# Weight pieces of 1024 columns instead of 2048 in a two-layer hybrid trunk

## The chip, the cores and the metric

The kernel runs on one core of a Trainium2 chip. The metric is the device time of one execution in microseconds; the median of several runs counts. The engines named here are TensorE (PE; its weight loads are PEld), VectorE (DVE), ScalarE (ACT), GpSimd (POOL) and SyncE (SP), which issues most DMA transfers.

## The reference

The kernel computes `DEPTH` = 2 layers on 256 tokens of width 1024 in float32, then a last RMS norm:

```python
for l in range(DEPTH):
    x = x + 0.5 * swiglu(rmsnorm(x, g_ffn1[l]), w_ffn1_gu[l], w_ffn1_down[l])
    x = x + hybrid_mixer(rmsnorm(x, g_mix[l]), w_in[l], ..., w_out[l], cos, sin)
    x = x + 0.5 * swiglu(rmsnorm(x, g_ffn2[l]), w_ffn2_gu[l], w_ffn2_down[l])
return rmsnorm(x, g_final)
```

The feed-forward width is 2816. The mixer projects to three kinds of attention (six forgetting heads, five stick-breaking heads, five sparse heads whose keys are chosen by an indexer with a top-k of 64) and three gates; each branch is projected up to 1024 columns, gated, summed and projected once more. All weights, about 208 MB, are read from HBM once.

## The kernel before

**Weights.** Every weight matrix is cut into chunks of 256 to 512 columns (the list `chunks`, 101 of them), and a chunk along its rows into blocks of 128, called k. One DMA transfer brings up to four k-blocks of a chunk (eight if the chunk has 256 columns), at most 2048 columns of float32 per partition, into one of four buffers `raw` (`emit_raw`, L223). The first chunk is transferred in smaller parts (the `cuts` of L206) into a buffer of its own, `raw_first`, and the second chunk in parts of two, two and four k-blocks.

**Splits.** The matrix multiplies run in float16, three for each product: a weight is the sum of a high part `whi` and a low part `wlo`, and so are the activations (`xThi`, `xTlo`). `emit_piece` (L258) makes both parts of a piece by `split` (L249): ScalarE scales and rounds `raw` into `whi` (L251), and VectorE subtracts that from the scaled `raw` into `wlo` (L253) and also sums the low part for a check, which is read by a DVE_READ_ACCUMULATOR. A piece is what one such pair of instructions covers: here the whole of a transfer. There are seven pairs of buffers of 2048 columns (`HL_BUFS`, `PIECE`).

**Order.** `project_T` (L317) and `project` (L363) walk over the pieces of a chunk. At the start of each piece they call `advance` (L274), which emits the splits up to `HL_BUFS` pieces ahead and the transfers up to four ahead of the last split, so a split waits for the pair of buffers that TensorE has just finished with. Then come the matmuls, k by k; after every second k-block (every fourth where a chunk has at most 256 columns) and at the end of a piece, `background` (L307) runs one step of each pending side task: attention heads, indexer, norm statistics. The tile framework then fixes the order of the instructions on each engine when the program is built, from their order in the program and its own estimate of when they are ready; on the chip each engine works through its queue in that order.

**What else stands in the same queues.** VectorE and ScalarE also make the operands of the attention (`Ta`, `Wa`, `Tiq`: L818 to L836), softmax parts (`nxa` L1006, `pa` L786, `pTa` L1019), the stick-breaking weights (`eb` L1101), the top-k selection (L915, L916), the gated merge (`gt` L1174 and L1177, `mT` L1179 by way of L251 and L253), the residual and the norm's operands (`xT`, `xThi` L495, `xTlo` L496), and the gate products of the feed-forward (`s0`, L660). At the start `FirstNorm.begin` (L596) alternates the blocks of the first norm with the first splits, as long as fewer than `HL_BUFS` pieces are emitted.

**The check.** `Guard` (L59) keeps one column of sums for each split; `verdict` (L83) transposes them on TensorE 128 columns at a time and reduces them on VectorE near the end. If it fails, a second pass in higher precision (`wide`) follows; it doesn't run here.

Of the kernel before, what the change touches and what calls it, by code (L numbers as in the profile page):

```python
# [24 lines left out]
DEPTH = 2  # L25
# [92 lines left out]
@with_exitstack  # L118
def tile_trunk(ctx, tc, io, out):

    pool = ctx.enter_context(tc.tile_pool(name="gp", bufs=1))
    flag = pool.tile([P, 2], I32, tag="flag", name="flag")
    trunk(tc, io, out, flag)
    bad = tc.nc.values_load(flag[:1, :1], min_val=0, max_val=1)
    with tc.If(bad != 0):
        trunk(tc, io, out, None)
# [3 lines left out]
def trunk(ctx, tc, io, out, flag):  # L130


    nc = tc.nc
    wide = flag is None
    DT = F32R if wide else F16
    sw, sx, sy, sm = (1.0,) * 4 if wide else (SW, SX, SY, SM)
    cp = ctx.enter_context(tc.tile_pool(name="cp", bufs=1))
    wp = ctx.enter_context(tc.tile_pool(name="wp", bufs=1))
    sp = ctx.enter_context(tc.tile_pool(name="sp", bufs=1))
    pp = ctx.enter_context(tc.tile_pool(name="pp", bufs=1, space=PSUM))  # L140
    guard = None if wide else Guard(nc, cp, flag, 256, 80, 3 * DEPTH)

    def behind(i, *firsts):

# [51 lines left out]
            add("w_out", D, h * 512, 512)  # L196
        add_ffn("w_ffn2_gu", "w_ffn2_down")

    RAW, PIECE = 2048, 1024 if wide else 2048
    RAW_BUFS, HL_BUFS = (4, 6) if wide else (4, 7)  # L200
    raws, pieces, chunk_pieces = [], [], []
    for ci, (nm, l, r, c, n) in enumerate(chunks):
        nk = -(-r // P)
        rk = 4 if n > 256 else 8
        pk = rk // 2 if wide else rk
        cuts = [0, 1, 2, 3, 4, 6, 8] if ci == 0 else [0, 2, 4, 8] if ci == 1 else list(range(0, nk, rk)) + [nk]  # L206
        lst = []
        for k0, k1 in zip(cuts, cuts[1:]):
            ks = list(range(k0, k1))
            raws.append((ci, ks))  # L210
            for i in range(0, len(ks), pk):
                sub = ks[i:i + pk]
                lst.append(len(pieces))
                pieces.append((len(raws) - 1, i, len(sub), r // P if r % P else None, sub))
        chunk_pieces.append(lst)
        if ci == 0:
            cuts0 = len(raws)
# [1038 lines left out]
```

## Time and profile before

| | before |
|---|---|
| median of 3 runs | 1148.99 us (1148.11 to 1150.2) |
| the profiled execution | 1148.52 us |
| its span, first to last instruction | 1146.6 us |
| busy PE / DVE / ACT | 1114.1 / 773.9 / 617.6 us |
| `wlo` on VectorE, `whi` on ScalarE (from `raw`) | 217 and 217 instructions |
| DMA | 209.96 MB, mean 183 GB/s |

A busy engine is one that has an instruction at work; matmuls overlap, so a busy share near 100% means that TensorE hardly ever stands still, not that it is at its peak. A wait is idle time of an engine just before an instruction, put down to the instruction that released it last. What TensorE waits for can lengthen the time; what an engine with idle time waits for can't by itself.

### The profile page before, as it was taken

The page shows a single profiled execution, that of the slowest core. Times are in us where ns is not written, and L with a number is a line of the kernel's source. Part 1 is how long each engine was busy: PE and PEld are TensorE (multiplying, and loading weights), DVE is VectorE, ACT ScalarE, POOL GpSimd, SP SyncE. Part 2 cuts the span into 40 slices and gives each one's busy share as a digit, 9 for nine tenths or more (in the row PEclk, how much of TensorE's full clock was granted, in tenths as well). Part 3 has the DMA queues.
Part 4 walks back from the last instruction along what each step waited for, and adds up shares of the span by engine and source line. Part 5 has one row for each costly group of instructions (what it writes and reads, how often), then busy time and mean ns, then how long its engine had stood idle before and what let it go on. Part 6 is the DMA issues. An engine that isn't in the chain of part 4 may idle for free. (4 is left out here: it accounts for less than half of the span.)

```text
span 1146.6 us, 22811 instructions
## 1 busy us (share of the span) xinstructions
PE 1114.1 (97%) x9744; PEld 956.8 (83%) x9744; DVE 773.9 (67%) x1339; ACT 617.6 (54%) x832; POOL 10.0 (1%) x25
## 2 busy tenths in 40 slices
PE   8999999989999999999999999999999999999996
PEld 7888887777888888888888888868788888888765
DVE  6966656897576975565576474579966689565632
ACT  7735445677667554353454363366766665544420
POOL 0000000000000000000000000000000000000000
PEclk9999999999999999999999999999999999999998
DMA  9956655555333865476665565565543439545701
GB/s 324 357 169 219 207 172 165 189 186 172 109 107 123 269 230 170 163 243 200 219 188 180 164 225 175 179 191 191 175 129 111 148 115 321 180 143 199 248 29 41
DMA packets 118755, 209.96 MB, mean 183 GB/s; under 512 B 4802, under 2 KB 43892, under 8 KB 118644
## 3 DMA queue, kind: packets, MB, share of 16 engines
q1 hardware_dynamic: 118324, 207.88, 55.8%
q8 instruction: 78, 1.28, 0.5%
q10 hardware_dynamic: 320, 0.53, 0.1%
q14 instruction: 33, 0.27, 0.1%
HBM read 207.35 MB, written 1.05 MB: 182 GB/s over the span
## 5 line engine op out<-in xcount | busy, mean ns | idle before, releaser
L253 DVE SCALAR_TENSOR_TENSOR wlo<-raw,whi 128x2048 f16<-128x2048 f32 (+5 forms) x217 | 446.4, 2059 | 257.7 <-ACT whi L251 257.5
L339 PEld LDWEIGHTS <-whi 128*128 128x128 f16 x5504 | 536.8, 98 | 67.8 <-issue 4.9
L251 ACT ACTIVATE whi<-raw 128x2048 f16<-128x2048 f32 (+5 forms) x217 | 373.6, 1725 | 384.1 <-issue 95.7
L339 PEld LDWEIGHTS <-wlo 128*128 128x128 f16 x2768 | 270.8, 98 | 38.6 <-issue 4.9
L339 PE MATMUL gw_ffn_gu<-xTlof,whi 128*128 128x256 f16 x704 | 191.7, 273 | 1.2 <-DVE xTlof L496 1.2
L339 PE MATMUL gw_ffn_gu<-xThif,wlo 128*128 128x256 f16 x704 | 191.5, 273 | 1.4 <-DVE wlo L253 1.3
L339 PE MATMUL gw_ffn_gu<-xThif,whi 128*128 128x256 f16 x704 | 191.6, 273 | 0.9 <-DVE s0w_ffn_gu L660 0.9
L339 PE MATMUL uw_ffn_gu<-xThif,whi 128*128 128x256 f16 x704 | 191.9, 273 | 0.0
L339 PE MATMUL uw_ffn_gu<-xThif,wlo 128*128 128x256 f16 x704 | 191.9, 273 | 0.0
L339 PE MATMUL uw_ffn_gu<-xTlof,whi 128*128 128x256 f16 x704 | 191.9, 273 | 0.0
L339 PE MATMUL gt<-xThimx,whi 128*128 128x256 f16 x384 | 104.8, 273 | 0.0
L339 PE MATMUL gt<-xTlomx,whi 128*128 128x256 f16 x384 | 104.7, 273 | 0.0
L339 PE MATMUL gt<-xThimx,wlo 128*128 128x256 f16 x384 | 104.7, 273 | 0.0
L339 PE MATMUL d0w_ffn_down<-ahw_ffn_gu,whi 128*128 128x256 f16 x264 | 72.0, 273 | 0.0
L339 PE MATMUL d0w_ffn_down<-alw_ffn_gu,whi 128*128 128x256 f16 x264 | 72.0, 273 | 0.0
L339 PE MATMUL d0w_ffn_down<-ahw_ffn_gu,wlo 128*128 128x256 f16 x264 | 72.0, 273 | 0.0
L339 PE MATMUL d512w_ffn_down<-ahw_ffn_gu,whi 128*128 128x256 f16 x264 | 72.0, 273 | 0.0
L339 PE MATMUL d512w_ffn_down<-alw_ffn_gu,whi 128*128 128x256 f16 x264 | 72.0, 273 | 0.0
L339 PE MATMUL d512w_ffn_down<-ahw_ffn_gu,wlo 128*128 128x256 f16 x264 | 72.0, 273 | 0.0
L339 PE MATMUL in<-xThimx,wlo 128*128 128x256 f16 x176 | 48.0, 273 | 0.0
L339 PE MATMUL in<-xThimx,whi 128*128 128x256 f16 x176 | 48.0, 273 | 0.0
L339 PE MATMUL in<-xTlomx,whi 128*128 128x256 f16 x176 | 48.0, 273 | 0.0
(329 smaller groups left out, 1372.5 us busy)
## 6 DMA issues: line engine op xcount, KB each, us to landing
raw<-in_w_ffn_gu_dram SPq DMA_DIRECT2D x61, 1024.0 KB, 5.3
raw<-in_w_ffn_down_dram SPq DMA_DIRECT2D x39, 1024.0 KB, 5.1
raw<-in_w_in_dram SPq DMA_DIRECT2D x26, 1024.0 KB, 5.1
raw<-in_w_ffn_gu_dram SPq DMA_DIRECT2D x32, 768.0 KB, 4.7
raw<-in_w_in_dram SPq DMA_DIRECT2D x12, 768.0 KB, 4.4
raw<-in_w_out_dram SPq DMA_DIRECT2D x8, 1024.0 KB, 5.1
raw<-in_w_ffn_down_dram SPq DMA_DIRECT2D x7, 512.0 KB, 3.8
raw<-in_w_in_dram SPq DMA_DIRECT2D x4, 896.0 KB, 4.8
```

Source lines behind the costliest of these rows:

```text
L251: a = nc.scalar.activation(hv, src, AF.Copy, scale=scale)
L253: return a, nc.vector.scalar_tensor_tensor(lv, src, scale, plain(hv), op0=ALU.mult, op1=ALU.subtract, **more)
L339: m = nc.tensor.matmul(o, u, v[:, k, :], start=(k == 0 and q == 0 and b % 2 == 0), stop=(end and q == len(ops) - 1))
```

## The change

`PIECE` becomes 1024 columns in this pass too, and `HL_BUFS` 14 instead of 7: a transfer of up to 2048 columns is now split in two pieces of half as many k-blocks, each with its own `whi` and `wlo` instruction and its own pair of buffers. `advance` is called at each of the smaller pieces. Transfers and `raw` buffers stay as they are. The sums of the check get room for 512 splits.

```diff
-    guard = None if wide else Guard(nc, cp, flag, 256, 80, 3 * DEPTH)
+    guard = None if wide else Guard(nc, cp, flag, 512, 80, 3 * DEPTH)
...
-    RAW, PIECE = 2048, 1024 if wide else 2048
-    RAW_BUFS, HL_BUFS = (4, 6) if wide else (4, 7)
+    RAW, PIECE = 2048, 1024
+    RAW_BUFS, HL_BUFS = (4, 6) if wide else (4, 14)
...
         rk = 4 if n > 256 else 8
-        pk = rk // 2 if wide else rk
+        pk = rk // 2
```

## Rows read from the trace of the kernel before

**Rows 1.** The page, part 1: busy us (share of the span) and instructions per engine.
```profile
PE 1114.1 (97%) x9744; PEld 956.8 (83%) x9744; DVE 773.9 (67%) x1339; ACT 617.6 (54%) x832; POOL 10.0 (1%) x25
```

**Rows 2.** TensorE's waits: who waited for whom: us in total, times, longest us.
```profile
PE sa L860 <- ACT pa L786: 4.1, 2, 2.1
PE o L339 <- DVE mT L253: 2.8, 2, 1.4
PE is L860 <- DVE Tiq L819: 2.3, 2, 1.2
PE sa L860 <- DVE Wa L836: 1.9, 2, 1.2
PE sb L860 <- DVE eb L1101: 1.9, 2, 0.9
...
PE gw_ffn_gu L339 <- DVE wlo L253: 1.3, 3, 0.6
PE gw_ffn_gu L339 <- DVE xTlof L496: 1.2, 3, 0.8
PE ya L990 <- ACT pTa L1019: 1.0, 2, 0.5
PE gw_ffn_gu L339 <- DVE s0w_ffn_gu L660: 0.9, 1, 0.9
...
PE sc L860 <- ACT pa L786: 0.7, 2, 0.4
```

**Rows 3.** Timeline of TensorE: start us, us, instruction [idle before <- releaser].
```profile
15.71 0.28 PE L339 MATMUL gw_ffn_gu<-xThif,wlo 128*128 128x256 f16 x1 [0.60 <-DVE wlo L253]
```

**Rows 4.** Timelines of VectorE and TensorE, first layer's attention.
```profile
248.34 2.29 DVE L253 SCALAR_TENSOR_TENSOR wlo<-raw,whi 128x2048 f16<-128x2048 f32 x1
...
250.67 0.42 DVE L1006 TENSOR_REDUCE nxa<-sa 128x1 f32<-128x256 f32 x1
...
251.75 0.39 PE L860 MATMUL sa<-Wa,Ta 128*128 128x256 f32 x1 [2.07 <-ACT pa L786]
```

**Rows 5.** Timeline of VectorE, second layer, between the merge and the output projection.
```profile
941.56 2.28 DVE L253 SCALAR_TENSOR_TENSOR wlo<-raw,whi 128x2048 f16<-128x2048 f32 x1
...
943.77 0.68 DVE L253 SCALAR_TENSOR_TENSOR mT<-gt,mT 128x512 f16<-128x512 f32 x1
```

**Rows 6.** Groups on VectorE by form: count | busy us, mean ns | idle before, releaser.
```profile
L253 DVE SCALAR_TENSOR_TENSOR wlo<-raw,whi 128x2048 f16<-128x2048 f32 x134 | 306.3, 2289 | 139.7 <-ACT whi L251 139.6
L253 DVE SCALAR_TENSOR_TENSOR wlo<-raw,whi 128x1536 f16<-128x1536 f32 x58 | 101.9, 1757 | 78.2 <-ACT whi L251 78.2
...
L253 DVE SCALAR_TENSOR_TENSOR wlo<-raw,whi 128x1024 f16<-128x1024 f32 x9 | 11.0, 1224 | 9.6 <-ACT whi L251 9.6
```

**Rows 7.** Timeline of VectorE: splits with no idle time between them and the next.
```profile
17.51 1.22 DVE L253 SCALAR_TENSOR_TENSOR wlo<-raw,whi 128x1024 f16<-128x1024 f32 x1
...
18.65 0.48 DVE L496 SCALAR_TENSOR_TENSOR xTlof<-xpf,gT,xThif 128x256 f16<-128x256 f32 x1
...
945.20 2.29 DVE L253 SCALAR_TENSOR_TENSOR wlo<-raw,whi 128x2048 f16<-128x2048 f32 x1
...
947.41 2.29 DVE L253 SCALAR_TENSOR_TENSOR wlo<-raw,whi 128x2048 f16<-128x2048 f32 x1
```

**Rows 8.** Windows: length, busy us of PE, PEld, DVE, ACT, POOL; clock, DMA share, GB/s.
```profile
225.00:250.00 25.00, 24.68 (x225) 21.58 (x223) 24.60 (x63) 18.25 (x34) 0.00 (x0) 1.00 0.62 207
375.00:400.00 25.00, 23.46 (x214) 20.90 (x215) 24.85 (x33) 15.14 (x14) 0.00 (x0) 1.00 0.81 266
```

**Rows 9.** Windows 225:250, 375:400, 787:812, 937:962, instructions on `wlo` alone, their sum.
```profile
sum 100.00, PE 75.30 PEld 26.15 DVE 51.31; mean PE 18.83 PEld 6.54 DVE 12.83
```

**Rows 10.** Groups on ScalarE by form, columns as in rows 6.
```profile
L251 ACT ACTIVATE whi<-raw 128x2048 f16<-128x2048 f32 x134 | 255.2, 1910 | 219.8 <-issue 51.6 <-PE uw_ffn_gu L339 35.8 <-PE gw_ffn_gu L339 34.0
```

**Rows 11.** Timelines of TensorE and VectorE near the end: the check of the sums.
```profile
1123.04 0.38 PE L92 MATMUL verdict<-ident,sums 128*128 128x128 f32 x2
1123.26 0.27 PE L374 MATMUL d0768w_ffn_down<-whi,ahw_ffn_gu 128*128 128x256 f16 x1
...
1127.51 0.16 DVE L115 TENSOR_SCALAR flag<-verdict 128x2 int32<-128x2 f32 x1 [1.53 <-PE verdict L114]
```

## The prediction

> **What bounds the kernel now.** First the page: TensorE is busy 97% of the 1146.6 us span [rows 1], so only what shortens or lengthens TensorE's own waits can move the time. The change adds work on VectorE and ScalarE and takes none from TensorE: the order in which the matrix multiplies are emitted, and the places where background steps are interleaved, come out the same, because a step falls after every second k-block (every fourth in narrow chunks), which is exactly where the new pieces end. So I read TensorE's waits next [rows 2]. The reader is to see who is *not* there: a wait for `wlo`, the last product of a weight split, appears three times for 1.3 us, and the longest of them is in the first 16 us [rows 3], where the pieces have 512 or 1024 columns already and stay as they are. After that weights are always ready before use. What is there: waits for small products of the attention, the merge and the norms (scores, softmax, `Tiq`, `Wa`, `eb`, `mT`, `xTlo`), made by VectorE and ScalarE between weight splits.
>
> Then I looked at what stood ahead of those products on their engine. At 248.34 VectorE starts a `wlo` of 2048 columns; the row maximum `nxa` behind it starts at 250.67, the exponential on ScalarE follows, and TensorE, which needs the score bank, stands 2.07 us at 251.75 [rows 4]. At 941.56 another `wlo` starts, and `mT`, which the output projection awaits, comes only at 943.77 [rows 5]. This pattern, a split for which TensorE is not waiting ahead of something needed at once, I found ahead of nine of the ten rows of rows 2 (all but the `wlo` one), 18 single waits in all.
>
> **The pieces.** By the code, 223 splits become 431: the 134 of 2048 columns and 58 of 1536 [rows 6] and 16 of 1280 to 1792 are cut in two, 208 cuts. DMA transfers into `raw` stay 1 MB and 223 in number, and the bytes held in `whi` and `wlo` stay the same. A `raw` buffer comes free when its second half is split, about when it did before.
>
> **What a cut costs.** A `wlo` of 2048 columns lasts 2.289 us, one of 1024 1.224 us, so a cut adds 0.16 us by durations [rows 6]. Back to back, where the end of one lies under the next, two of 2048 start 2.21 us apart (945.20, 947.41), and after one of 1024 the next operation starts 1.14 us later (17.51, 18.65) [rows 7]: a cut then adds 0.07 us. 208 cuts are 15 to 33 us on VectorE. Over the whole span VectorE is busy 67% [rows 1], and TensorE does not wait for weights; in the feed-forward stages, where VectorE has idle time and the fourteen buffers are a lead of seven transfers, the cost lies beside TensorE's matmuls and I take nothing for it. If that cover were gone, `wlo` would appear in the waits, with at most 0.16 us a cut. It isn't hidden where VectorE is full: 24.60 us of 25 in 225:250 and 24.85 in 375:400 [rows 8], and the same two stretches of the second layer. `wlo` takes 51.3 us in these four, over 2.3 us a piece 22 to 23 pieces [rows 9]. If each cut there ends at TensorE, it costs 23 x 0.07 = 1.6 to 23 x 0.16 = 3.7 us; if the small products are ordered ahead of the second halves, nothing. I take half of the low end, 0.8 us, because two of the four stretches (merge and output) contain few products on which TensorE waits.
> ScalarE pays per cut too, but is less full than VectorE (18.25 and 15.14 us of 25 in the same stretches); its 2048-column `whi` of 1.91 us [rows 10] becomes two of about 0.95 us by halving it, an estimate from that row. Behind a `whi` stand the exponentials, so the shorter block helps there as on VectorE. I count it in the same waits, not again.
>
> **What a cut gives.** Where one half stands ahead of a product that TensorE awaits, and the other half comes after it, the product is 2.21 - 1.14 = 1.07 us earlier. Where both halves still stand ahead, nothing is gained. From above, each wait gives the smaller of itself and 1.07 us [rows 2]: `sa` for `pa` 2.1, `o` for `mT` 2.1, `is` for `Tiq` 2.1, `sa` for `Wa` 1.8, `sb` for `eb` 1.1 (a 1536-column piece, 1.76 - 1.22 = 0.53 each), `gw` for `xTlo` 1.2, `ya` for `pTa` 1.0, `gw` for `s0` 0.9, `sc` for `pa` 0.7. Together 13.0 us; from below 0.
> Of these, the waits where the awaited product (or the one that feeds it at once) stood right behind the split are `sa`-`pa`, `mT`, `xTlo`, `pTa`, `s0` and `sc`: 8.0 us. In the others (`Tiq`, `Wa`, `eb`, 5.0 us) several VectorE operations lie between, in stretches that are full anyway, and a queue that is never empty ends no earlier for being cut finer; I take 0 for them. Of the 8.0 I take two thirds, 5.3 us. The code is the reason for more than half: each half is emitted at its own half-piece of TensorE's work with a background step in between, and its buffer is freed half a piece at a time, so the halves reach VectorE apart. The reason for less than all: at the later half-step the fourteen buffers reach half a piece further ahead than the seven did, and both halves of a transfer that has only just landed are ready together.
>
> **The edges.** At the start the first eight pieces keep their size, but fourteen buffers let more of them be prepared ahead; the first wait for `s0` (0.9 us) could grow by one half, 1.1 us, or vanish. I keep it among the waits above. The check of the weight sums gets four transposes on TensorE instead of two: two took 0.22 us (1123.04 to 1123.26), so +0.2 us on the path to the end. Its VectorE sums become 256 columns longer and two reductions more, about 1.2 us, beside VectorE's idle 1.53 us before the flag [rows 11]; if that cover is gone, up to 1.2 us.
>
> **The rule that speaks against it.** VectorE's rows in 225:250 show a full engine [rows 8]. The Trainium skill, Perfetto Trace Analysis, section Optimizing Scalar/DVE Operations, says that each such operation carries a fixed access overhead, about 60 ns on VectorE from SBUF, and that larger operations are better when the engine is saturated, while breaking them up may help when it isn't and causes bubbles elsewhere. By its 60 ns the 23 cuts would cost an estimated 1.4 us instead of 1.6. By its first half this kernel gets slower, by its second faster; it is full in four stretches and not in the rest, so the first half is my slower rival below.
>
> **The sum.** -5.3 + 0.8 + 0.2 = -4.3 us. The profiled execution took 1148.52 us, 1.9 us of it outside its span, and lies 0.5 us under the median of the runs, 1148.99. Its own forecast is 1144.2; for the median, 1144.7.
>
> **The rivals.**
> - *Most of the bound comes true* (chance 0.12): the halves also loosen the full stretches, because small products that were not yet ready when a long split began now get in between. For it: the same engine work, smaller blocks. Against it: the 24.6 us of 25. -10 to -12 us, 1137 to 1139.
> - *The change doesn't do what it says for the queues* (chance 0.24): the order on each engine is fixed when the program is built, and both halves stand together ahead of the products as the whole did. Gain up to 2, cost 0.8 to 2: 1147 to 1150. For it: at 945.20 and 947.41 two whole splits already stand together [rows 7].
> - *VectorE as the bound* (chance 0.17): in the four full stretches each cut reaches TensorE at 0.07 to 0.16 us, 1.6 to 3.7 us with 0.2 of the check, and where the lookahead grew by half a piece one more half (1.1 us) stands ahead of a product at a few places, say two. 1148.99 + 1.8 to + 6.1: 1150.8 to 1155. It decides if less than about 2 of the 8.0 us are realised. For it: the full stretches, where the maxima of the top-k selection queue with the splits. Against it: most of the 18 waits are shorter than one whole block.
>
> **How the numbers follow.** Forecast, 1141 to 1146.5: 0.47. With the rivals' 0.12, 0.24 and 0.17 that is 1. What a measurement can tell from no change is about 0.2%, 2.3 us here. Faster by more than that (below 1146.7): 0.47 + 0.12 = 0.59, and nearly none of the rest; within it: 0.24 and a little of the slower case, 0.26; slower: 0.15. The range leaves out the lowest part of the first rival and the upper part of the last, a tenth each: 1138.5 to 1152.
>
> **What would show it.** Right: in the profile after, 425 `wlo` groups apart from the first chunk, nearly all at 1.22 us or below; VectorE's busy time 15 to 33 us higher; no new row of waits for `wlo`; the 2.1 us of `sa` for `pa` and the 1.4 us of `o` for `mT` down to about 1 and 0.4. Wrong by the second rival: pairs of 1.14 us apart directly ahead of the same `nxa` and `mT`. Wrong by the third: the sums of `Tiq`, `Wa` and `eb` grow, with VectorE above 24.6 of 25 in stretches that are longer than before. It would also be wrong if the finer emission moved something I read as fixed, the order of the attention steps on TensorE or the first normalisation's place in ScalarE's queue.

## The result and the profile after

The changed kernel takes 1141.95 us (median of 4 runs, 1141.66 to 1145.33), the kernel before 1149.6 us on the same chip (median of 4, 1148.11 to 1152.39). The ratio is 0.9938, interval 0.9924 to 0.9951: 5.6 to 8.7 us faster. The forecast was 1144.7 with a range of 1138.5 to 1152. One execution of a kernel below (`e8_quarter`) took 1938.75 us at a granted clock of 0.556, where its other four had 0.994 to 0.997; its ratio is that of the four.

Two executions of the changed kernel were profiled. The first took 1145.33 us, the second (a rerun in a later group of runs, `e10_changed_again` below) 1140.65 us. They are told apart here, because the first holds an accident that the second doesn't. Page of the first, part 1, as in [rows 1]:

```profile
PE 1113.5 (97%) x9746; PEld 960.4 (84%) x9746; DVE 799.3 (70%) x1757; ACT 649.8 (57%) x1040; POOL 12.5 (1%) x25
```

And of the second:

```profile
span 1138.9 us, 23671 instructions
...
PE 1108.9 (97%) x9746; PEld 958.1 (84%) x9746; DVE 798.7 (70%) x1757; ACT 649.6 (57%) x1040; POOL 12.5 (1%) x25
```

VectorE does 25 us more than in [rows 1], ScalarE 32 us more, TensorE two instructions more, and the end comes earlier. VectorE's groups by form (first execution) answer to [rows 6]:

```profile
L253 DVE SCALAR_TENSOR_TENSOR wlo<-raw,whi 128x1024 f16<-128x1024 f32 x291 | 352.8, 1223 | 155.5 <-ACT whi L251 154.5
L253 DVE SCALAR_TENSOR_TENSOR wlo<-raw,whi 128x768 f16<-128x768 f32 x88 | 84.1, 957 | 69.5 <-ACT whi L251 67.4
L253 DVE DVE_READ_ACCUMULATOR wlo<-raw,whi 128x1 f32 x425 | 35.3, 83 | 0.0
```

TensorE's waits in the second execution answer to [rows 2]:

```profile
PE sa L860 <- ACT pa L786: 4.4, 2, 2.2
PE ya L990 <- ACT pTa L1019: 2.3, 2, 2.0
PE is L860 <- DVE Tiq L819: 2.2, 2, 1.1
...
PE sc L860 <- ACT pa L786: 1.7, 2, 0.9
PE o L339 <- DVE mT L253: 1.6, 2, 0.9
PE gw_ffn_gu L339 <- DVE s0w_ffn_gu L660: 1.4, 1, 1.4
PE sb L860 <- DVE eb L1101: 1.3, 2, 0.7
PE gw_ffn_gu L339 <- DVE wlo L253: 0.9, 2, 0.6
PE yc L990 <- ACT pTc L1019: 0.7, 2, 0.3
PE gw_ffn_gu L339 <- DVE s1w_ffn_gu L660: 0.7, 1, 0.7
PE o L339 <- ACT mT L251: 0.6, 2, 0.4
```

The reader is to see two things. The list is not the list of before with smaller numbers: `sa` for `Wa` and `gw` for `xTlo` are gone, `sa` for `pa` is about as long as it was (4.4, 4.1 before), `ya`, `sc`, `s0` are longer and `yc`, `s1` are new. And the sum doesn't add up: span less busy TensorE is 1146.6 - 1114.1 = 32.5 us before and 1138.9 - 1108.9 = 30.0 us here. Idle time accounts for 2.5 of the 7.7 us by which the span is shorter.

**A better ledger.** A matmul's busy time in the profile reaches beyond the point at which the next one could start (0.27 us long, started every 0.11 us), so a late start first eats that overlap and only the rest is a wait. I therefore worked out from TensorE's timeline, for every matmul, how much longer after its predecessor it started than is usual (the median) for that predecessor's form, and added up what exceeds 0.02 us by the operand it was released by. Microseconds:

| late starts of TensorE, by releaser | before | changed, 2nd execution | difference |
|---|---|---|---|
| all | 43.23 | 35.88 | -7.35 |
| `sa` for `Wa` | 2.21 | 0 | -2.21 |
| `ppa`, `ppc` for `pa`, `pc` | 2.41 | 0 | -2.41 |
| `gw` for `xTlo`, `in` for `xThi`, `xTlo` (norms) | 3.00 | 0 | -3.00 |
| `o` for `gt` | 0.87 | 0 | -0.87 |
| `gw` for `wlo`, `whi` | 2.32 | 1.27 | -1.05 |
| `sb` for `eb` | 2.20 | 1.65 | -0.55 |
| `o` for `mT` | 3.16 | 2.91 | -0.25 |
| `is` for `Tiq` | 2.65 | 2.49 | -0.16 |
| `sa` for `pa` | 4.47 | 4.75 | +0.28 |
| `sc` for `pa` | 1.03 | 2.08 | +1.05 |
| `ya` for `pTa` | 1.58 | 2.63 | +1.05 |
| `gw` for `s0`, `s1` (start) | 1.05 | 2.35 | +1.30 |
| `yc`, `qc` for `pTc` | 0 | 1.51 | +1.51 |
| the rest, by releaser | 1.14 | 0.30 | -0.84 |
| no releaser shown (lower clock among it) | 15.14 | 13.94 | -1.20 |

This ledger explains 7.35 of the 7.7 us. By stage (profile against profile), between the first weight matmuls of the stages (both layers together): the first three `w_in` chunks -1.8, the attention -2.5, the last four gate chunks -2.1, `up` -0.9, `out` -0.25, first chunks of the feed-forwards -1.6, the start +1.05, the check of the sums +0.2, the rest of the feed-forwards 0.0.

**What moved in the attention.** The place of [rows 4] in the first changed execution, TensorE, then VectorE, then ScalarE:

```profile
247.47 0.28 PE L151 MATMUL sa<-c_mask_a,identb 128*128 128x128 bf16 x2
249.97 0.43 PE L860 MATMUL sa<-Wa,Ta 128*128 128x256 f32 x1 [2.23 <-ACT pa L786]
...
248.72 0.42 DVE L1006 TENSOR_REDUCE nxa<-sa 128x1 f32<-128x256 f32 x1
249.17 1.23 DVE L253 SCALAR_TENSOR_TENSOR wlo<-raw,whi 128x1024 f16<-128x1024 f32 x1
...
248.42 1.05 ACT L251 ACTIVATE whi<-raw 128x1024 f16<-128x1024 f32 x1
249.37 0.46 ACT L786 ACTIVATE pa<-sa,nxa 128x256 f32<-128x256 f32 x1
```

`nxa` now stands ahead of the split (248.72; 250.67 in [rows 4]), and `sa` comes at 249.97 instead of 251.75. Its wait is no shorter, because TensorE's order changed too: before, eleven `in` matmuls stood between the two `sa` groups; now they come after the second group. The wait is met earlier, and what was late behind it (`ppa`, `Wa`) is no longer late. This place alone does not show what a shorter block gives: the kernel of run 5, which cuts nothing and is slower than before, has the same move.

**The accident in the first execution.** ScalarE, VectorE and TensorE at the first layer's output projection (start, length, instruction, idle before and releaser):

```profile
377.96 2.00 ACT L251 ACTIVATE whi<-raw 128x1024 f16<-128x1024 f32 x2 [7.37 <-DMA raw<-in_w_ffn_gu_dram]
379.87 1.13 ACT L251 ACTIVATE mT<-gt 128x512 f16<-128x512 f32 x2
...
380.52 0.69 DVE L253 SCALAR_TENSOR_TENSOR mT<-gt,mT 128x512 f16<-128x512 f32 x1 [1.92 <-ACT mT L251]
...
380.54 0.37 PE L339 MATMUL o<-mT,whi 128*128 128x256 f16 x1 [2.67 <-ACT mT L251]
```

And the window behind it (length, busy PE, PEld, DVE, ACT, POOL, then granted clock, DMA share, GB/s):

```profile
379.90:386.70 6.80, 5.80 (x27) 3.88 (x27) 6.18 (x13) 3.11 (x5) 0.00 (x0) 0.50 0.37 111
```

ScalarE stands 7.37 us before a split of the next feed-forward's weights, whose transfer has not landed, and `mT`, which TensorE needs, stands behind it in the queue. TensorE waits 2.67 us and then runs at 0.50, the lower of its two levels, for 6.8 us. The stage is 4.5 us longer than before. In the second execution the same two splits stand in the same place, but the transfer lands sooner:

```profile
375.79 2.00 ACT L251 ACTIVATE whi<-raw 128x1024 f16<-128x1024 f32 x2 [4.91 <-DMA raw<-in_w_ffn_gu_dram]
377.70 1.13 ACT L251 ACTIVATE mT<-gt 128x512 f16<-128x512 f32 x2
...
378.36 0.27 PE L339 MATMUL o<-mT,whi 128*128 128x256 f16 x1 [0.40 <-ACT mT L251]
...
379.37 0.27 PE L339 MATMUL o<-mT,whi 128*128 128x256 f16 x1 [0.73 <-DVE mT L253]
```

There the stage is 0.1 us shorter than before.

### The profile page after: what moved, and what is told of

The parts are those of the page before. It is cut to its first block, busy times and chain, and to the rows that moved or that the text cites. A ratio compares the mean times of both kernels' runs of the same rounds, so it can differ in the third digit from the quotient of the medians.

```text
span 1143.5 us, 23671 instructions
## 1 busy us (share of the span) xinstructions
PE 1113.5 (97%) x9746; PEld 960.4 (84%) x9746; DVE 799.3 (70%) x1757; ACT 649.8 (57%) x1040; POOL 12.5 (1%) x25
## 3 DMA queue, kind: packets, MB, share of 16 engines
HBM read 207.35 MB, written 1.05 MB: 182 GB/s over the span
## 4 chain that ended last, share of the span: by engine, by line
PE 77%; DVE 13%; ACT 6%; issue 2%; DMA 1%; POOL 0%; POOLq 0%; DVEq 0%; ACTq 0%
PE gw_ffn_gu L339 19%; PE uw_ffn_gu L339 19%; PE d512w_ffn_down L339 8%; PE d0w_ffn_down L339 8%; PE gt L339 6%; DVE wlo L253 5%; PE o L339 3%; ACT whi L251 2%; PE in L376 2%; PE in L374 1%; PE in L375 1%; DMA raw<-in_w_ffn_gu_dram 1%; ACT gt L1162 1%; PE in L339 1%; DVE gt L1174 1%
## 5 line engine op out<-in xcount | busy, mean ns | idle before, releaser
L253 DVE SCALAR_TENSOR_TENSOR wlo<-raw,whi 128x1024 f16<-128x1024 f32 (+6 forms) x425 | 476.2, 1128 | 258.7 <-ACT whi L251 255.5
L251 ACT ACTIVATE whi<-raw 128x1024 f16<-128x1024 f32 (+6 forms) x425 | 411.4, 978 | 378.9 <-PE uw_ffn_gu L339 93.4
L339 PE MATMUL o<-mT,whi 128*128 128x256 f16 x256 | 45.1, 282 | 4.2 <-ACT mT L251 3.2
```

The source lines that it names most:

```text
L251: a = nc.scalar.activation(hv, src, AF.Copy, scale=scale)
L253: return a, nc.vector.scalar_tensor_tensor(lv, src, scale, plain(hv), op0=ALU.mult, op1=ALU.subtract, **more)
L339: m = nc.tensor.matmul(o, u, v[:, k, :], start=(k == 0 and q == 0 and b % 2 == 0), stop=(end and q == len(ops) - 1))
```

## The experiments

Two theories stood against each other after the result. A: the cut helps because halves are emitted at different moments and reach VectorE apart (the reason on record). B: it helps merely because a block in the queue is shorter, wherever it was emitted. Theory C is that a deeper lookahead counts, and D that any edit reshuffles the queues and the time scatters. Beside them stood the question of the price, which the forecast took as 0.8 us, and of the lookahead, which the change halves in columns per buffer but not in columns in all. Differences in microseconds are the ratio's interval on the 1150 us of the kernel before, with the ratio as the middle, or profile against profile where that is said.

**1. Both instructions cut, seven whole buffers kept.** Both halves are emitted together, at the place of the whole.

```diff
-    guard = None if wide else Guard(nc, cp, flag, 256, 80, 3 * DEPTH)
+    guard = None if wide else Guard(nc, cp, flag, 512, 80, 3 * DEPTH)
...
-        r = split(hv, lv, src, sw, guard and guard.weight())
+        h = (4 if n > 256 else 8) // 2
+        parts = [(0, nk)] if wide or nk <= h else [(0, h), (h, nk)]
+        pa, pv = (parts if True else [(0, nk)]), (parts if True else [(0, nk)])
+        r0 = [nc.scalar.activation(hv[:, s:e], src[:, s:e], AF.Copy, scale=sw) for s, e in pa]
+        r1 = [nc.vector.scalar_tensor_tensor(lv[:, s:e], src[:, s:e], sw, plain(hv[:, s:e]), op0=ALU.mult,
+                                             op1=ALU.subtract, **({} if guard is None else {"accum_out": guard.weight()}))
+              for s, e in pv]
+        r = (r0[-1], r1[-1])
```

> Buffers, lookahead and the place of emission as before (7 pairs of 2048 columns), but each whi and each wlo is issued as two instructions of half the size at the same place in the program. Theory A (small products get in between halves that reach the engines apart): in the program's order the two halves stand next to each other nearly everywhere, so most of the gain is missing, -2.5 to +1.5 us against before. Theory B (blocks of half the size are enough by themselves, because wlo starts half a whi earlier): most of the gain, -5 to -8 us. Theory C (the deeper lookahead of fourteen buffers is what counts): no gain, 0 to +2 us. Theory D (any change reshuffles the queues and the time scatters): anything between -8 and +4 us, with no relation to the parts.

Measured: 1143.55 us, ratio 0.9945 (0.9931 to 0.9958), 4.8 to 7.9 us faster. Most of the gain is there without emitting the halves apart. In the trace, 205 to 400 us, VectorE has 32 splits before, which stand in 30 uninterrupted blocks; here 65 halves in 44 blocks, in the changed kernel 64 in 52. So halves that are emitted together are still pulled apart in 14 places by the order that is fixed when the program is built. One of them is the place of [rows 4], VectorE and then TensorE:

```profile
248.42 1.23 DVE L273 SCALAR_TENSOR_TENSOR wlo<-raw,whi 128x1024 f16<-128x1024 f32 x1
...
249.68 0.42 DVE L1013 TENSOR_REDUCE nxa<-sa 128x1 f32<-128x256 f32 x1
250.02 1.22 DVE L273 SCALAR_TENSOR_TENSOR wlo<-raw,whi 128x1024 f16<-128x1024 f32 x1
...
250.76 0.39 PE L867 MATMUL sa<-Wa,Ta 128*128 128x256 f32 x1 [3.01 <-ACT pa L793]
```

`nxa` starts 1.26 us after the split ahead of it (2.33 in [rows 4]), 1.07 us less, which is the step that the forecast reckoned with, and `sa` comes 0.99 us earlier than in [rows 4]. The number of such places doesn't set the gain by itself: with VectorE alone cut (run 2) there are 49 blocks, more than here, and a smaller gain. Theory A is refuted as far as it says that the apart emission is needed; it adds 8 more such places and, by this run against the changed kernel, perhaps 1 us, inside the intervals. How the waits are redistributed shows again that single rows don't tell the gain:

```profile
PE sa L867 <- ACT pa L793: 6.0, 2, 3.0
PE o L346 <- DVE mT L253: 2.6, 2, 1.3
```

`sa` for `pa` is 1.9 us longer than in [rows 2] in a kernel that is 6 us faster, because the `in` matmuls that stood ahead of the second `sa` come after it here too, and `Tiq` doesn't appear in its list at all.

**2. One engine cut at a time.** The same edit with `parts` only in `pv` (VectorE), and only in `pa` (ScalarE; the sums keep their 256 columns).

> As before, but only wlo on VectorE is issued as two halves, at the same place; whi stays whole. Theory A: -1.5 to +1.5 us, VectorE's queue holds both halves together. Theory B: half of the gain or less, since wlo can't start before the whole whi ends: -3 to 0 us. Theory C: 0 to +2 us.

> As before, but only whi on ScalarE is issued as two halves, at the same place; wlo stays whole. Theory A: -1.5 to +1 us. Theory B: -1 to +1 us, wlo still waits for both halves and is as long as before. Theory C: 0 to +1 us.

Measured: VectorE alone 1146.25 us, 0.9966 (0.9954 to 0.9978); ScalarE alone 1148.57 us, 0.999 (0.9981 to 0.9999). The first is some 3.9 us faster, the second 1.1, together 5.0 against the 6.3 us of run 1. The middle for VectorE alone lies beyond every range expected (3 at most), the one for ScalarE in A's and just past B's. The gain is on VectorE for the larger part: the norm operands' late starts at the second layer's first chunk (0.93 us) go with the VectorE cut alone and stay with the ScalarE cut alone.

**3. The lookahead.** Halves with 12 and with 10 pairs of buffers, and whole pieces with 6 pairs instead of 7.

```diff
-    RAW_BUFS, HL_BUFS = (4, 6) if wide else (4, 14)
+    RAW_BUFS, HL_BUFS = (4, 6) if wide else (4, 12)
```

> The changed kernel (pieces of 1024 columns, emitted apart) with twelve pairs of buffers instead of fourteen: the lookahead is half a piece to a piece of 2048 columns shorter than that of before. Theory A: the gain stays, -5 to -8.5 us against before, a little more if VectorE's full stretches get lighter. Theory C: the gain is lost, -1 to +3 us. Theory D: anything between -8 and +4 us.

> The changed kernel with ten pairs of half pieces. If fewer splits ahead keep whi that waits for a transfer from standing ahead of mT and other products on ScalarE, the gain goes on or stays: -8.5 to -11 us against before. If ten are too few, wlo appears in TensorE's waits at the merge and output stage, where the lead was shortest, and the gain shrinks: -3 to -7 us.

> The kernel before, whole pieces of 2048 columns, with six pairs of buffers instead of seven: the lookahead of the run with twelve half pieces, without the cut. If the shorter lookahead by itself is what made twelve better than fourteen, this is faster than before by about as much, -1 to -2.5 us. If twelve was better because of where half pieces fall, there is no such gain here: -0.7 to +2 us.

Measured: 12 pairs 1141.06 us, 0.9923 (0.991 to 0.9937); 10 pairs 1142.92 us, 0.9943 (0.993 to 0.9955); whole pieces with 6 pairs 1151.91 us, 1.0023 (1.0013 to 1.0033). A shorter lookahead by itself costs 1.5 to 3.8 us with whole pieces, more than the 2 us expected at most, and run 1 gains with the buffers of before, so the gain is not one of lookahead. Among the halves, 10, 12 and 14 pairs lie within 2 us, in no order; the intervals of 12 and 14 overlap. The 6.6 us of ten pairs lie where "ten are too few" had them, but not for its reason: `wlo` is waited for 0.9 us in all, as with fourteen. Whole pieces with more than seven pairs were not run.

**4. The price: first try, misplaced.** 208 small VectorE instructions, one per split that the change cuts, without a cut.

```diff
+        if not wide and nk > (4 if n > 256 else 8) // 2:
+            load = guard.sums[:, 240:242]
+            nc.vector.tensor_scalar(load, load, 1.0, None, op0=ALU.mult)
```

> The kernel before, whole pieces, with one small VectorE instruction (128 x 2) behind each of the 208 splits that the change cuts: the price of more instructions on VectorE without the smaller blocks. Their own rows in the trace before (128 x 2, 0.15 to 0.17 us, about 0.1 us back to back) make 20 to 35 us of VectorE. Theory: hidden outside the full stretches, so -0.5 to +1.5 us against before. Rival (VectorE is the bound of the four full stretches, 23 pieces there): +2.3 to +4 us.

Measured: 1159.4 us, 1.0084 (1.0071 to 1.0097). It says nothing of the price, because the instructions did not depend on the splits and all 208 ran in the first 99 us. VectorE's timeline at the start:

```profile
1.15 13.11 DVE L272 TENSOR_SCALAR sums<-sums 128x2 f32<-128x2 f32 x62 [1.15 <-POOL sums L68]
```

And the wait of TensorE that came of it:

```profile
PE xpf L588 <- DVE gT L422: 8.8, 1, 8.8
```

10.4 of the 10.8 us, profile against profile, lie ahead of the first layer's projections.

**5. The price, in place.** The instruction now reads the low part that the split has just made.

```diff
+        if not wide and nk > (4 if n > 256 else 8) // 2:
+            nc.vector.tensor_scalar(guard.sums[:, 240:242], lv[:, 0, :2], 1.0, None, op0=ALU.mult)
```

> The kernel before with whole pieces, plus 208 small VectorE operations (128x2, reading the low part just made, into spare columns of the sums that nothing reads), each bound to stand behind a split that the change would cut. This is the price of the extra VectorE instructions without any gain of finer blocks. Each should last about 0.17 us as the earlier ones did (35.6 us for 208), which is the upper price of a cut. Theory (the price is hidden except in the full stretches): -0.5 to +1.5 us against the kernel before. Rival (VectorE as the bound: each of the 23 added ones in the full stretches reaches TensorE): +2.3 to +4 us.

Measured: 1151.83 us, 1.0015 (1.0006 to 1.0024): 0.7 to 2.8 us. The group on VectorE:

```profile
L271 DVE TENSOR_SCALAR sums<-wlo 128x2 f32<-128x2 f16 x208 | 34.1, 164 | 3.3
```

And in the timeline one of these instructions with the next one behind it:

```profile
244.23 0.16 DVE L271 TENSOR_SCALAR sums<-wlo 128x2 f32<-128x2 f16 x1
244.30 0.42 DVE L917 MAX8 m<-isc 128x8 f32<-128x256 f32 x1
```

Each lasts 0.16 us and holds the next up by 0.07, the two prices that [rows 6, 7] gave for a cut, so this is near the price of 208 cuts on VectorE with none of their gain (ScalarE's is not in it). The middle, 1.7 us, is just above "hidden" (-0.5 to +1.5) and under "VectorE as the bound" (+2.3 to +4); the interval touches both. By stage it lies at the first three `w_in` chunks (+1.2), in the attention (+0.9, of which -0.6 comes back in the last gate chunks), `up` and `out` (+0.65 and +0.7) and where the feed-forwards begin (+0.4 at the start, +0.1 to +0.3 at the other three), and not at all in the 600 us of the feed-forwards' inner chunks (0.0). Profile against profile the difference is larger, 3.9 us, but the profiled execution of before is one of its quicker ones, so the timed runs decide.

It is not the price alone, since TensorE's order moved here too. At the place of [rows 4], VectorE and then TensorE:

```profile
250.13 0.42 DVE L1008 TENSOR_REDUCE nxa<-sa 128x1 f32<-128x256 f32 x1
250.59 2.29 DVE L253 SCALAR_TENSOR_TENSOR wlo<-raw,whi 128x2048 f16<-128x2048 f32 x1
...
251.21 0.39 PE L862 MATMUL sa<-Wa,Ta 128*128 128x256 f32 x1 [1.89 <-ACT pa L788]
```

`nxa` stands ahead of a whole split and the two `sa` groups next to each other, as in the changed kernel. That bears on theory D. By the traces, about 150 of the 9744 matmuls stand elsewhere in TensorE's queue than before, in the kernel with ScalarE alone cut about 130, with six pairs about 215: none of these has shorter blocks on VectorE, and they came out 1.7 us slower, 1.1 faster and 2.6 slower. The kernels whose VectorE blocks are cut have some 220 to 270 moved and are 3.9 to 11.2 us faster, all of them. So in these three the moves, with whatever else was changed, came to between -1.1 and +2.6 us, which is no rival for the gain of the others; how much of it they carry in one kernel isn't separated.

**6. Finer still.** Pieces of 512 columns, 24 pairs of buffers; the places of the background steps stay those of the changed kernel. The sums of the first pieces are overwritten by later ones.

```diff
-    RAW, PIECE = 2048, 1024
-    RAW_BUFS, HL_BUFS = (4, 6) if wide else (4, 14)
+    RAW, PIECE = 2048, 1024 if wide else 512
+    RAW_BUFS, HL_BUFS = (4, 6) if wide else (4, 24)
...
-        pk = rk // 2
+        pk = rk // 2 if wide else rk // 4
...
```

> Pieces of 512 columns in 24 pairs of buffers (the bytes of twelve half pieces), background steps at the same k-blocks as before; the sums of the first pieces are overwritten by later ones, so the check covers only the last 512 splits. Blocks of a quarter: if the wait behind a block is what counts, a further 2 to 4 us over the run with twelve half pieces: -10 to -13 us against before. If the price of the cuts has caught up (each 1024 columns cut again for 0.07 to 0.16 us, about 46 more cuts in the full stretches, 3 to 7 us), no further gain or a loss: -3 to -8.5 us.

Measured: 1140.51 us (median of all five), 0.9914 (0.99 to 0.9928). The middle, 9.9 us faster, lies between the two cases expected (10 to 13 if the blocks go on counting, 3 to 8.5 if the price has caught up). Then the same with a lookahead of 12 pieces while the first 16 are used:

```diff
-        while state["piece"] < min(state.get("hold", len(pieces)), i + HL_BUFS):
+        ahead = HL_BUFS if wide or i >= 16 else 12
+        while state["piece"] < min(state.get("hold", len(pieces)), i + ahead):
```

> Pieces of 512 columns in 24 pairs of buffers, as in the run with quarter pieces, with the lookahead limited to 12 pieces during the first 16 pieces (the sums of the first pieces are overwritten by later ones, so the check covers fewer of them). Theory: the quarter pieces lost about 1 us in the first two chunks because more splits stood ahead of the first gate products; with a shorter lookahead there this comes back, 0.5 to 1.5 us faster than the quarter pieces, -9.5 to -12 us against the kernel before. Rival: 12 small pieces are too little at the start, TensorE waits for wlo there, and nothing or less than nothing comes back.

Measured: 1139.24 us (1139.1 to 1139.33), 0.9903 (0.9888 to 0.9917), the best of all: 9.5 to 12.9 us faster than before, and at the start 1.0 us better than the quarter pieces without it, profile against profile. Its busy VectorE is 842 us, 68 us above [rows 1]. So whatever price the further cuts have, it is smaller than what finer blocks still give. Two of its waits:

```profile
PE sa L864 <- ACT pa L790: 5.3, 4, 2.3
...
PE o L340 <- DVE mT L253: 0.3, 2, 0.2
```

Against the changed kernel's rerun, `out` is 2.25 us shorter (`o` for `mT` 0.3 instead of 1.6 + 0.6), the start 0.7, the last gate chunks 0.6, the first `w_in` chunks 0.4; the attention is 2.7 us longer, 0.2 above the kernel before. Whether the cuts are paid there isn't shown: VectorE is busy 75.0 of the attention's 82.5 us per layer, and in `out`, which became shorter, all of 21.3.

**7. The changed kernel again, and the accident taken away.** The rerun tells chance from system; the other kernel holds back the splits of the next feed-forward until `mT` is emitted and binds the first of them behind the last `mT` in ScalarE's queue.

> The changed kernel once more, with a second profile. If the 4.5 us lost at the first output projection, where ScalarE stood before a transfer ahead of mT, was a late transfer of that one execution, the stage takes no longer than before, the profiled execution is near the others, 1142 us, and the ratio stays near 0.993. If it belongs to the kernel, the profile shows the ScalarE wait again with TensorE waiting 2 us or more for mT, and the profiled execution is near 1145 us.

Measured: 1141.74 us, 0.9935 (0.992 to 0.995), profiled at 1140.65 without the accident. One of its six executions took 1147.34 us, so something of that size does come back now and then; whether it was this wait can't be told, as it has no trace.

```diff
+                if h and b == 0 and not wide:
+                    state["hold"] = chunk_pieces[state["chunk"] + 5][0]
...
-                            split(mh[:, k:k + 2, :], ml[:, k:k + 2, :], v0, sm, note())
+                            last = split(mh[:, k:k + 2, :], ml[:, k:k + 2, :], v0, sm, note())[0]
+                if h and b == 2 and not wide:
+                    del state["hold"]
+                    state["mT"] = last
...
+        if "mT" in state:
+            behind(r[0], state.pop("mT"))
```

> The changed kernel, with the splits of the next feed-forward's weights held back until the four mT splits are emitted, and in ScalarE's queue bound to stand behind the last of them; in the first layer all four mT then stand ahead of the six splits that stood between them, in the second layer only the splits behind the feed-forward's first are moved. Theory (a split that stands ahead of mT delays it, and by its transfer's wait where it is late): TensorE's wait for mT in the first layer goes from 0.5 to 2.7 us to under 0.3, the output stage of the first layer gets 0.4 to 0.8 us shorter than in the undisturbed changed kernel, and no granted clock of 0.5 follows it. The price is that six splits come later; lookahead covers it. Whole: 1140.5 to 1142. Rival (mT is late because of VectorE's own queue, not ScalarE's): the wait for mT stays at 0.5 us or more with VectorE named, whole 1141.5 to 1143.

Measured: 1142.22 us, 0.9926 (0.9913 to 0.9939), the same as the changed kernel. The part that was aimed at came true, and it was given back behind it. ScalarE and TensorE:

```profile
380.47 1.23 ACT L251 ACTIVATE mT<-gt 128x512 f16<-128x512 f32 x2 [10.57 <-DVE gt L1181]
...
381.88 0.27 PE L341 MATMUL o<-mT,whi 128*128 128x256 f16 x1 [0.33 <-DVE mT L253]
...
403.83 0.27 PE L341 MATMUL gw_ffn_gu<-xTlof,whi 128*128 128x256 f16 x1 [0.83 <-DVE xTlof L498]
```

No transfer stands between ScalarE and `mT` any more (the 10.57 us are idle time in front of the product itself), `o` waits 0.33 us (under 0.3 was expected), and the output stage is 1.0 us shorter per layer than in the undisturbed changed kernel. But the next feed-forward's first chunk is 1.0 us longer per layer: `gw` waits for `xTlo` again, a wait that had been gone. The splits that came late and now fill VectorE's queue ahead of it are the likely reason; I didn't follow them one by one. "Lookahead covers it" was wrong.

This kernel's profiled execution (1145.4 us) also shows the accident at another place, the start: ScalarE before two late transfers.

```profile
28.58 2.00 ACT L251 ACTIVATE whi<-raw 128x1024 f16<-128x1024 f32 x2 [1.73 <-DMA raw<-in_w_ffn_gu_dram]
...
33.32 2.00 ACT L251 ACTIVATE whi<-raw 128x1024 f16<-128x1024 f32 x2 [1.51 <-DMA raw<-in_w_ffn_gu_dram]
```

`gw` then waits 2.3 us for `s1`, which stands behind these splits, and the window after that wait is (columns as above)

```profile
38.20:41.60 3.40, 3.40 (x19) 2.33 (x17) 3.32 (x5) 3.40 (x6) 0.00 (x0) 0.51 0.94 336
```

In the rerun ScalarE had waited 0.59 us there and none at the second; the stretch is 3.3 us longer here. So the pattern, a split whose transfer may be late ahead of something that TensorE needs, exists at two places at least. At `mT` the order cures it, at a price that just cancels the gain of a normal execution.

## Why the prediction was right, and where it wasn't

**The total and the mechanism.** -4.3 us was forecast, -7.1 (5.6 to 8.7) came, inside the forecast's own case (1141 to 1146.5) and near its lower end. That finer blocks on VectorE, with small products between them, make the gain holds: it comes with the cut alone (run 1), mostly with VectorE's (run 2), not with the lookahead (run 3), and goes on with finer pieces (run 6). Kernels that were reordered without shorter blocks on VectorE (run 5) don't come near it.

**The pieces and their price.** 425 `wlo` groups outside the first chunk at 1.23 us or less, VectorE 25 us busier (15 to 33 forecast), no new row for `wlo`: all as said. The cost per cut, 0.07 to 0.16 us, was right. The cost at TensorE was taken as 0.8 with bounds of 1.6 to 3.7 if every cut in the four full stretches counted; run 5 gives 1.7 (0.7 to 2.8), with the moved order in it and ScalarE's cuts not. "Nothing" outside the full stretches was right for the feed-forwards' inner chunks, but by run 5's stages wrong where `w_in`, `up` and the feed-forwards begin: VectorE is not full there (22.5 of 28.2 us in the first `w_in` chunks before), yet TensorE waits for single products of it. With the price back in, the gain of the finer blocks is about 7.1 + 1.7 + 0.2 = 9.0 us (an estimate from these runs), where 5.3 was taken. That the transfers are 1 MB holds for those of 2048 columns only; no term hangs on it.

**Which waits would go: mostly wrong.** The forecast took two thirds of 8.0 us from the "direct" waits (`sa` for `pa`, `mT`, `xTlo`, `pTa`, `s0`, `sc`) and nothing from the "indirect" (`Tiq`, `Wa`, `eb`). In the ledger the direct ones together (with `s1`) are 1.7 us *longer*, although `xTlo` lost 1.7; the indirect ones are 2.9 us shorter, `Wa` alone 2.2; and 5.6 us come from small late starts that the forecast didn't list (`ppa`, `ppc`, the mixer's norm operands, `gt`, first-chunk splits), while `yc` and `qc` took 1.5 back. Of the two waits named as the sign, `mT` went from 1.4 us a layer to 1.1 instead of 0.4. Two steps failed.
- *That the order of the matrix multiplies comes out the same.* The order in which they are emitted does; the order in TensorE's queue, fixed when the program is built, doesn't. Even run 1, which changes nothing in their emission, has some 230 of them elsewhere, and the second `sa` moved ahead of eleven `in` matmuls. So the 2.1 us of `sa` for `pa` did not fall to 1; its place moved forward by 1.8 us instead. The last sentence of the forecast names this as what would make it wrong.
- *The list of waits as the upper bound.* Idle time leaves out the overlap that a late start eats first: 43.2 us of late starts stood against 32.5 us of idle time, and several of the starts that were cured hardly show in the list of waits (`ppa` and `ppc`: 2.4 us in the ledger, 0.8 as idle time).

That these errors cancelled and the total fell into the range is luck. The sign is not: every kernel with shorter blocks on VectorE gained. That a chain of small products is as long as the blocks ahead of it allow, and that the order decides which matmul shows the wait, fits the traces; apart from the place in run 1 it wasn't followed product by product.

**Emitted apart.** The reason for "more than half" was the apart emission; run 1 shows that the order does most of it without.

**The edges.** The start was named as a risk of one half, 1.1 us: `s0` and `s1` are 1.3 us later in the ledger. In the rerun three halves stand back to back on VectorE ahead of `s0` (28.55 to 31.99); run 6 got 1.0 us back with a shorter lookahead there. The four transposes of the check take 0.43 us between the last weight matmuls (1115.11 to 1115.54 in the second execution), 0.21 more than two; 0.2 was forecast.

**The rule against it.** VectorE is full in stretches (24.2 of 25 us in 225:250 after), and yet the finer cut gained, and a still finer one too. So the half of the rule in the Trainium skill (Perfetto Trace Analysis, section Optimizing Scalar/DVE Operations) that favours larger operations on a saturated engine did not decide: `out`, where VectorE is busy 22.4 of 22.5 us before, became 0.1 us shorter per layer with halves and 1.25 with quarters. Its other half, that breaking up may help where the engine is not saturated and causes bubbles elsewhere, fits the first `w_in` chunks, 0.9 us shorter per layer.

## What to carry over

On engines that work through their queues in order, cut large work that nobody waits for into smaller blocks, even when the engine is full in places: the price came to 1.7 us for 208 more instructions on VectorE, and the gain stayed above it down to a quarter of the original size, though not in every stage. Judge such a change by stage lengths and by late starts of the bounding engine, not by the rows of its wait list, which rearrange themselves. And look for non-urgent work that may wait for a transfer ahead of an urgent product: it cost nothing in one profiled execution and 4.5 us in the other, and moving it later took the time from the next product behind it.

## What the runs showed of the hardware that I had not expected

A lower clock isn't always a loss. In the first changed execution TensorE's granted clock is 0.50 after the wait at 249.97, in the second it is 1.00 over the same window; the next `nxa`, on VectorE, comes at nearly the same time in both. Window of the first, then of the second:

```profile
250.20:253.60 3.40, 3.40 (x17) 2.33 (x17) 3.40 (x17) 2.47 (x5) 0.00 (x0) 0.50 0.59 163
```

```profile
250.20:253.60 3.40, 3.40 (x29) 2.84 (x30) 3.40 (x15) 2.47 (x5) 0.00 (x0) 1.00 0.54 149
```

VectorE's timeline, first and second execution:

```profile
253.88 0.28 DVE L1006 TENSOR_REDUCE nxa<-sa 128x1 f32<-128x128 f32 x1
```

```profile
253.99 0.28 DVE L1006 TENSOR_REDUCE nxa<-sa 128x1 f32<-128x128 f32 x1
```

TensorE does 17 matmuls instead of 29 in that window and pays nothing: VectorE is busy all 3.40 us in both, and the layer's attention is as long in the first as in the second execution (both 1.3 us shorter than before). At 379.9 and at 38.2 the same level, together with the wait before it, went with stages 4.5 and 3.3 us longer. The level also does not follow the wait's length alone: both executions had waited 2.2 us (2.23 and 2.22).

The larger tile of sums shows at the very start: `warm` waits 2.0 us for POOL's `ident` in all kernels with 512 sums and 1.8 us in those with 256, because POOL clears the sums first. That it costs time isn't shown: the first weight matmul comes 0.17 us later than before in run 1 with 512 sums and in the ScalarE cut with 256 alike. Its timeline in the second execution:

```profile
0.74 0.59 POOL L68 MEMSET sums<- 128x592 f32 x1 [0.29 <-POOLq L1244]
1.26 0.20 POOL masks.py:197 MEMSET ident<- 128x128 f32 x1
```

In the kernel before it takes 0.38 us for 336 columns, and `ident` starts at 1.05.
